# TensorE transposes for a few blocks of an attention layer, and output stores issued by SyncE

## Chip, cores and metric

The kernel runs on one core of one Trainium2 chip. A core has TensorE (PE, matrix products into PSUM), VectorE (DVE), ScalarE (ACT), GpSimd (POOL) and SyncE (SP, which here issues DMAs), and 16 DMA engines that all queues of the core share. Each engine executes its own instruction list in order and waits for the others by semaphores. The metric is device time in microseconds (us); less is better.

## What is computed

A decoder trunk of two layers over 2048 tokens of width 1024, in float32. Layer A is a gated linear recurrence; layer B is attention over a sliding window of 128 tokens, with 16 query heads of 64 and 2 shared key/value heads. The change concerns layer B alone:

```python
k, v = ...                            # computed once from layer A's output: projection, RMS norm per key head
h = rmsnorm(x, norm_g)
u = h @ w_in                          # 1024 -> 1024 queries | 1024 gates
q = rmsnorm(q per head, q_norm_g)
s = q @ k.T * scale + alibi           # per block of 128 queries: the block and the one before it, masked
p = exp(s - max) ; p = p / (sum(p) + exp(sink - max))
y = (p @ v) * silu(gate)
out = x + y @ w_out
```

## The kernel before

Every float32 operand is split into two float16 parts, hi and lo, and a product is three float16 passes (hi hi, hi lo, lo hi), accumulated in PSUM. Layer B works on 16 blocks of 128 tokens. For block b TensorE does:

- `project(b)`: keys and values (24 matmuls of 256 columns), then queries (48 of 512 columns); `project_gate(b)`: 48 of 512 columns; `finish(b)`: the output projection, 48 of 512 columns, which needs the transposed gated values `yT`.
- `scores(b, n)` for the two halves n of the heads (16 matmuls of 256 columns in 4 pairs of heads), which need the transposed queries `qT`; `values(b, n)` (32 small matmuls), which need the transposed exponentials `pT` and a masked copy of them that GpSimd makes.

A product needs its left operand with the contraction on the partitions, so normalized input, keys, queries, exponentials and gated values are transposed. All of these transposes are DMA transposes, issued on SyncE's queue by `flip` (line 321): per block one for xT, kT, qT and yT and two for pT; block 15 has two half ones for yT, since `finish(15)` is done in two parts. The block's residual input is loaded by SyncE (`fetch_chain`, line 1580, four buffers); the finished block is stored by GpSimd's queue (`x_add`, line 1888), except for block 15, whose halves SyncE stores (line 1885).

The order of the work is made at build time. `Plan` (line 81) holds the expected times of five engines. Each chain of steps (`q_chain`, `softmax`, `gate_chain`, ...) is a generator that yields what it will use, as `yield DVE_, 1220, 1` for an expected 1220 ns of DVE, `yield SP_, 1900` for the issue of a transpose, `yield None, 2500` for its landing, or a `Flag` to wait for. When several steps could begin, the one that can begin first goes first, and `RANK` breaks ties. TensorE is fed by two streams (`run`, line 142): `attention()` with scores and values, and `others()` with projections, gates and finishes; the first goes ahead whenever its flags are set by then, plus `SLACK` ns of margin. `LEAD`, `GAPS` and `TIMES` say how much TensorE time of the other stream has to pass before a step of attention may come; `LATER` moves `finish(12)`, `finish(13)` and `finish(14)` back in the order of the other stream. `end_plan` ties each engine's instructions to the order of the plan; on the chip an engine keeps that order whatever the real times are.

```python
seq.append(("finish", b - 1))               # 1540, behind project(b + 1) and gate(b + 1)
yield slot("s", 3), PAIR                    # 1487, one of 3 PSUM buffers for a pair of heads
yield SP_, 1900                             # 1783, in softmax
flip(ph.rearrange("p w h n -> p (w h n)"), pT.rearrange("p w h n -> p (w h) n"))
yield None, 2500
```

With `LATER = (1, 0, 1)` the end of the other stream is project(15), finish(12), gate(15), finish(13), finish(14), finish(15). `yT` has two buffers, so that block 14's is block 12's, and is free when `finish(12)` has been done. The gated values of all blocks pass through one buffer (`yS`), and so do their hi and lo parts (`yhl`).

Of the kernel before, what the change touches and what calls it, by code (L numbers as in the profile page):

```python
# [36 lines left out]

LEAD = 9353  # L40
PAIR, GAPS = 440, (1000, 800)
TIMES = ((4259, 2588, 17865, 17829), (2559, 6794, 2129, 5953), (19559, 3400, 24653, 13594), (14447, 15300, 0, 6800))
LATER = (1, 0, 1)


RANK = (4, 5, 3, 0, 1, 4, 2, 5, 3, 4, 0, 3, 5, 2)
SLACK = 300
LATE5 = 200
LO_POOL = (1, 2)

# [126 lines left out]
def trunk(ctx, tc, x, wA, gw, par, gains, woA, wkv, wB, woB, vec, alib, out):  # L177
# [12 lines left out]
    psum = [psA.enter_context(tc.tile_pool(name="psA", bufs=1, space=bass.MemoryType.PSUM))]  # L190


    id16 = xp.tile([P, P], F16, name="id16")
    make_identity(nc, id16)
    id32 = xp.tile([P, P], F32, name="id32")
    make_identity(nc, id32)
# [1280 lines left out]
    def scores(b, n):  # L1477
        d = st[b]
        yield [F["qT"][b], F["kT"][b]], 0
        if n == 0:  # L1480
            for k in ("rl", "lsum", "mr", "mt", "bi", "sk"):
                d[k] = col(k, HEADS)
            d["parts"] = 2 if b == NB - 1 else 1
        qT, kt = d["qT"], d["kT"]
        left = [4]
        for hp in range(4 * n, 4 * n + 4):
            yield slot("s", 3), PAIR
            o = pst([P, 2, 2 * P], F32, "s", uniq("s"), 3)
            free = taken("s")
            for i in range(2):  # L1490
                h = 2 * hp + i
                for w in range(2):
                    mm(o[:, i], qT[:, h], kt[:, h // 8, w].rearrange("p r n -> p (r n)"), w == 0, w == 1)
            plan.go(evacuate(b, n, hp, o, free, left), RANK[0])
            yield GAPS[0]
        H["s"][2 * b + n].set()
# [75 lines left out]
            f.set()  # L1572


    def fetch_chain(b):
        if b >= 4:
            yield st[b - 4]["stored"]
        yield SP_, 300
        xb = p3.tile([P, D], F32, tag="x1", name=uniq("x1"), bufs=4)
        nc.sync.dma_start(xb, x1D[b])  # L1580
        st[b]["x1"] = xb
        yield None, 3300
        F["x1"][b].set()

    def norm_chain():
# [27 lines left out]
    def kv_chain(b, kv, free):  # L1613
        d = st[b]
        yield ACT_, 650
        kn = p3.tile([P, 2, HD], F32, tag="kn", name=uniq("kn"), bufs=1)
        kss = col("kss", 2)
        for h in range(2):
            act.activation(kn[:, h], kv[:, h * 64 : h * 64 + 64], AF.Square, accum_out=kss[:, h : h + 1])
        yield DVE_, 230, 1  # L1620
        kva = col("kva", 2)
        dve.tensor_scalar(kva, kss, 1.0 / HD, epsk, ALU.mult, ALU.add)
        yield POOL_, 720
        rk = col("rk", 2)
        pool.tensor_tensor(rk, kva, mhalf[:, 0:2], ALU.pow)
        yield DVE_, 500
        for h in range(2):
            dve.scalar_tensor_tensor(kn[:, h], kv[:, h * 64 : h * 64 + 64], rk[:, h : h + 1], gk, ALU.mult, ALU.mult)
        yield ACT_, 270

        v32 = p3.tile([P, 2, HD], F32, tag="v32", name=uniq("v32"), bufs=2)
        act.activation(v32, kv[:, 128:256].rearrange("p (h d) -> p h d", h=2), AF.Copy, scale=2.0**-21)
        d["v32"] = v32
        free.set()
        plan.go(v_chain(b), RANK[10])
        yield ACT_, 500
        kd = p3.tile([P, 2, 2, 2, HD], F16, tag="kd", name=uniq("kd"), bufs=1)
        for r in range(2):
            act.copy(kd[:, :, 0, r], kn)
        yield POOL_, 900, 1  # L1640
        for r in range(2):
            pool.tensor_tensor(kd[:, :, 1, r], kn, kd[:, :, 0, 0], ALU.subtract)
        if b >= 2:
            yield H["s"][2 * b - 3]
        yield SP_, 1200
        kt = p3.tile([P, 2, 2, 2, P], F16, tag="kT", name=uniq("kT"), bufs=2)
        flip(kd.rearrange("p h w r d -> p (h w r d)"), kt.rearrange("p h w r n -> p (h w) r n")[:, :, 1, :])
        d["kT"] = kt
        yield None, 1700
        yield POOL_, 620, 1  # L1650
        if b == 0:
            pool.memset(kt[:, :, :, 0, :], 0.0)
        else:
            pool.tensor_copy(kt[:, :, :, 0, :], st[b - 1]["kT"][:, :, :, 1, :])
        F["kT"][b].set()
# [34 lines left out]
    def q_chain(b):  # L1690
        d = st[b]
        yield d["qparts"][0]
        yield d["qparts"][1]
        sq = qhS.rearrange("p h r d -> p (h r d)").bitcast(F32)
        qn, qh = qnS, qhS
        yield DVE_, 1210
        qss = col("qss", HEADS)
        dve.tensor_reduce(qss, sq.rearrange("p (h d) -> p h d", d=HD), AX.X, ALU.add)
        yield DVE_, 230, 1
        qva = col("qva", HEADS)  # L1700
        dve.tensor_scalar(qva, qss, 1.0 / HD, epsq, ALU.mult, ALU.add)
        yield POOL_, 2920
        rq = col("rq", HEADS)
        pool.tensor_tensor(rq, qva, mhalf, ALU.pow)
        yield POOL_, 220, 1
        rq2 = col("rq2", HEADS)
        pool.tensor_tensor(rq2, rq, qsc, ALU.mult)
        yield POOL_, 1900, 1
        pool.tensor_tensor(qn, qn, rq2.unsqueeze(2).to_broadcast([P, HEADS, HD]), ALU.mult)
        yield ACT_, 1050  # L1710
        act.copy(qh[:, :, 0], qn)
        yield DVE_, 1200, 1
        dve.tensor_tensor(qh[:, :, 1], qn, qh[:, :, 0], ALU.subtract)
        if b:
            yield H["s"][2 * b - 1]
        yield SP_, 1900
        qT = p3.tile([P, HEADS, P], F16, tag="qT", name=uniq("qT"), bufs=1)
        flip(qh.rearrange("p h r d -> p (h r d)"), qT)
        F["q"][b].set()
        d["qT"] = qT  # L1720
        yield None, 2900
        F["qT"][b].set()

    def g_part(b, n, o, free):
# [30 lines left out]
    def softmax(b, n):  # L1755
        s, d = sS, st[b]
        hs, i = bsf(n), 2 * b + n
        mr, mt, bi, sk, lsum, rl = (d[k][:, hs] for k in ("mr", "mt", "bi", "sk", "lsum", "rl"))
        vec = vecs[:, 128 + 8 * n : 136 + 8 * n]
        yield DVE_, 500, 1  # L1760
        dve.tensor_tensor(mt, mr, ssc[:, hs], ALU.mult)
        dve.tensor_tensor(mt, mt, vec, ALU.max)
        dve.tensor_scalar(bi, mt, -1.0, LN2_15, ALU.mult, ALU.add)  # L1763
        for h in range(8 * n, 8 * n + 8):
            yield ACT_, 480, 0, "exp"
            act.activation(  # L1766
                s[:, h],
                s[:, h],
                AF.Exp,
                bias=d["bi"][:, h : h + 1],  # L1770
                scale=ssc[:, h : h + 1],
                accum_out=d["lsum"][:, h : h + 1],
            )
        plan.go(row_sums(b, n), RANK[12])
        ph, pT = phS[n], pTs[n]
        if b:
            yield H["pv"][i - 2]
        yield DVE_, 700, 1
        dve.tensor_copy(ph[:, 0], s[:, hs])  # L1779
        yield DVE_, 1220, 1  # L1780
        dve.tensor_tensor(ph[:, 1], s[:, hs], ph[:, 0], ALU.subtract)  # L1781
        H["cut"][i].set()
        yield SP_, 1900
        flip(ph.rearrange("p w h n -> p (w h n)"), pT.rearrange("p w h n -> p (w h) n"))
        yield None, 2500
        H["pT"][i].set()
        for w in range(2):

            yield POOL_, 1090, 1
            pool.affine_select(ph[:, w], pT[:, w], [[0, 8], [-1, P]], ALU.is_gt, 0.0, base=0, channel_multiplier=1)  # L1790
        H["pU"][i].set()
# [38 lines left out]
    def gate_chain(b, i):  # L1830
# [24 lines left out]
        yh = yhl[:, 2 * i * n : 2 * (i + 1) * n]  # L1855
        if b and i == 0:
            yield F["yh"][b - 1]
        yield ACT_, 1150 / parts
        act.activation(yh[:, 0:n], yi, AF.Copy, scale=syb)
        yield DVE_, 1285 / parts, 1  # L1860
        dve.scalar_tensor_tensor(yh[:, n : 2 * n], yi, syb, yh[:, 0:n], ALU.mult, ALU.subtract)  # L1861
        if i == parts - 1:
            F["yfree"][b].set()
        if b >= 2 and i == 0:
            yield F["out"][b - 2]
        yield SP_, 1900
        if i == 0:
            d["yTt"] = p3.tile([P, 2 * KD, P], F16, tag="yT", name=uniq("yT"), bufs=2)
            d["yTp"] = flag()
        m = 2 * KD // parts  # L1870
        F["yh"][b].set()
        flip(yh, d["yTt"][:, i * m : (i + 1) * m])
        yield None, 2700
        (F["yT"][b] if i == 0 else d["yTp"]).set()

    def x_add(b, n, p, o, free):
# [5 lines left out]
        if d["parts"] == 2:  # L1882
            if p == 1:
                yield SP_, 300
                nc.sync.dma_start(out[b * P : (b + 1) * P, n * CH : n * CH + CH], sl)
        elif n == 1:
            yield POOL_, 640
            pool.dma_start(out[b * P : (b + 1) * P, :], d["x1"])
            yield None, 3300
            d["stored"].set()  # L1890

    for b in range(NB):
# [81 lines left out]
```

## Time and profile before

| | us |
|---|---|
| median of 3 runs (1538.58 to 1542.13) | 1538.91 |
| the profiled execution, its own time | 1536.42 |
| its span | 1534.7 |
| layer A and weights, up to TensorE's first matmul of layer B | 873.6 |
| layer B, from there to TensorE's last matmul | 657.1 |
| from there to the end of the span | 4.0 |

| engine | busy us | share of the span |
|---|---|---|
| TensorE | 1496.4 | 98% |
| VectorE | 1027.4 | 67% |
| ScalarE | 887.8 | 58% |
| GpSimd | 421.8 | 27% |

Busy time is the time in which an instruction of the engine was in flight. On an engine that is busy nearly throughout, what is left to look for are the few places where it waits, and how fast it runs; on the others, idle time matters only where TensorE waits for them. The granted clock is TensorE's, as a share of full speed.

### The profile page before, as it was taken

The numbers are of one execution on the slowest core, as the hardware profiler recorded it, in microseconds if no ns is written. First come the engines' busy times: TensorE is split into PE (matmuls) and PEld (weight loads), VectorE is DVE, ScalarE is ACT, GpSimd is POOL, SyncE is SP. The second block draws the span as 40 slices with busy tenths as digits, with TensorE's granted clock in tenths as the row PEclk, the third lists the DMA queues.
The fourth block names the chain that finished last, engine by engine and source line by source line (L and its number), as shares of the span: only waits on it lengthen the run. The fifth ranks groups of instructions, "written<-read, shape, count | busy, mean of one in ns | idle before, by whom it ended". The sixth has DMA issues, their size and how long they took to land. (4 is left out here: it accounts for less than half of the span.)

```text
span 1534.7 us, 23073 instructions
## 1 busy us (share of the span) xinstructions
PE 1496.4 (98%) x8503; PEld 746.8 (49%) x8503; DVE 1027.4 (67%) x2221; ACT 887.8 (58%) x1773; POOL 421.8 (27%) x578
## 2 busy tenths in 40 slices
PE   5999999999999999999999999999999999999997
PEld 5444444444444444444444455555555555555553
DVE  7578878778777766963247246766657656756774
ACT  6678667767766757510145167665556646646761
POOL 2232111111111121100000135544344444454532
PEclk9999999999999999999999999999999999999998
DMA  6664122022143212796258334444434544454434
GB/s 195 161 169 104 34 80 68 26 82 66 28 149 122 83 61 88 263 331 244 104 186 293 126 70 85 102 90 97 100 87 100 88 95 100 77 120 90 90 70 96
DMA packets 242545, 177.27 MB, mean 116 GB/s; under 512 B 205056, under 2 KB 215552, under 8 KB 242432
## 3 DMA queue, kind: packets, MB, share of 16 engines
q1 hardware_dynamic: 233984, 146.95, 37.0%
q0 software_dynamic: 8304, 28.84, 5.5%
q8 instruction: 66, 1.08, 0.3%
q14 instruction: 47, 0.39, 0.1%
q10 hardware_dynamic: 144, 0.01, 0.0%
HBM read 92.93 MB, written 29.36 MB: 80 GB/s over the span
## 5 line engine op out<-in xcount | busy, mean ns | idle before, releaser
L275 PEld LDWEIGHTS <-w 128*128 128x128 f16 x2448 | 233.6, 99 | 269.0 <-issue 9.8
L275 PE MATMUL pm<-wq,xT 128*128 128x512 f16 x1536 | 340.3, 379 | 2.6 <-ACT gg L1728 2.6
L275 PEld LDWEIGHTS <-xT 128*128 128x128 f16 x1920 | 186.7, 98 | 178.3 <-issue 2.8
L275 PE MATMUL pu<-xnT,w 128*128 128x512 f16 (+2 forms) x1296 | 259.4, 358 | 2.9 <-DMA xnT<-xs 1.9
L275 PE MATMUL pg<-xnT,w 128*128 128x512 f16 x1152 | 251.9, 379 | 0.0
L275 PE MATMUL po<-wo,xnT 128*128 128x512 f16 x1152 | 249.4, 379 | 0.5 <-ACT ri L744 0.5
L275 PEld LDWEIGHTS <-xnT 128*128 128x128 f16 x1152 | 112.6, 98 | 136.0 <-issue 0.9
L275 PE MATMUL pm<-xnT,yT 128*128 128x512 f16 x768 | 174.5, 382 | 1.6 <-DMA yT<-qy 1.6
L675 DVE SCALAR_TENSOR_TENSOR xc<-u,cwS,xc 128x512 f32<-128x512 f32 x144 | 110.7, 776 | 66.0 <-ACT xc L671 62.8
L1766 ACT ACTIVATE sq<-sq,bi,ssc 128x128 f32<-128x128 f32 x256 | 123.4, 486 | 7.2 <-DVE bi L1763 7.1
L275 PEld LDWEIGHTS <-yT 128*128 128x128 f16 x768 | 74.2, 98 | 86.4 <-DMA yT<-qy 1.7
L1739 ACT COPY sq<-s 128x256 f32<-128x256 f32 x128 | 47.2, 373 | 87.2 <-PE s L275 82.6
L300 ACT ACTIVATE xnT<-xnT,sy 128x1536 f16<-128x1536 f32 x14 | 22.0, 1570 | 128.4 <-PE po L275 128.4
L685 POOL TENSOR_TENSOR hl<-xc,hl 128x512 f16<-128x512 f32 x32 | 42.2, 1321 | 175.6 <-ACT hl L680 136.6
L734 ACT ACTIVATE gs<-pg,gsc 128x512 f32<-128x512 f32 x48 | 32.9, 688 | 95.9 <-DMA yD<-gs 68.7
L1741 DVE COPY_PREDICATED sq<-mask,s 128x256 f32<-128x256 int32 x128 | 53.0, 439 | 30.7 <-ACT sq L1739 29.6
L1750 DVE CUSTOM_DVE_ANT_0 sq<-sq,al 128x128 f32<-128x128 f32 x256 | 72.5, 329 | 0.1
L275 PE MATMUL pr<-hl,gw 128*128 128x512 f16 x288 | 68.2, 380 | 2.8 <-ACT gs L734 1.8
L744 ACT ACTIVATE ri<-pr,pr,rsc 128x512 f32<-128x512 f32 x96 | 69.4, 776 | 1.2 <-PE pr L275 0.7
L816 POOL DMA_DIRECT2D yD<-gs x48 | 36.8, 766 | 118.5 <-DVE gs L806 118.3
L275 PE MATMUL s<-kT,qT 128*128 128x256 f16 x512 | 67.2, 273 | 1.7 <-DMA qT<-qy 1.5
L1202 DVE SCALAR_TENSOR_TENSOR xnT<-po,cA,xnT 128x512 f32<-128x512 f32 x28 | 20.8, 748 | 70.6 <-PE po L275 70.6
(255 smaller groups left out, 2204.6 us busy)
## 6 DMA issues: line engine op xcount, KB each, us to landing
xnT<-in_wB_dram SPq DMA_DIRECT2D x32, 512.0 KB, 6.0
yD<-gs POOLq DMA_DIRECT2D x48, 256.0 KB, 2.8
st<-in_woA_dram SPq DMA_DIRECT2D x24, 512.0 KB, 4.3
xnT<-yD SPq DMA_DIRECT2D x16, 768.0 KB, 5.5
st<-in_wA_dram SPq DMA_DIRECT2D x15, 768.0 KB, 5.3
xs<-in_x_dram SPq DMA_DIRECT2D x16, 512.0 KB, 3.8
xnT<-in_x_dram SPq DMA_DIRECT2D x16, 512.0 KB, 5.0
x1D<-xnT POOLq DMA_DIRECT2D x16, 512.0 KB, 4.4
```

Of the source, the lines that this page charges most:

```text
L275: lastmm[0] = pe.matmul(o, lhsT, rhs, start=start, stop=stop, skip_group_check=True)
L300: act.activation(hi, src, AF.Copy, scale=scale)
L675: dve.scalar_tensor_tensor(xc, u[:, d : d + CH], cw[:, j, d : d + 1], xc, ALU.mult, ALU.add)
L685: (pool if j in LO_POOL else dve).tensor_tensor(hl[:, 1], xc, hl[:, 0], ALU.subtract)
L734: act.activation(gs, o, AF.Silu, scale=W["gsc"])
L744: act.activation(v, o[j], AF.Sigmoid, bias=pr[:, t0 + j, 5 + w : 6 + w], scale=W["rsc"])
L816: pool.dma_start(yD[4 * c : 4 * c + 4, :, t, :].rearrange("b p n -> p b n"), gs.rearrange("p (b n) -> p b n", n=P),)
L1202: dve.scalar_tensor_tensor(xs_, o[n], cA[:, c : c + 1], xs_, ALU.mult, ALU.add)
L1739: act.copy(sl, o[:, :, P:])
L1741: dve.copy_predicated(sl, mask.unsqueeze(1).to_broadcast([P, 2, P]), o[:, :, 0:P])
L1750: dve.tensor_tensor_reduce(s[:, h], s[:, h], al[:, i * P : (i + 1) * P], 1.0, -3.4e38, ALU.add, ALU.max, m)
L1766: act.activation(s[:, h], s[:, h], AF.Exp, bias=d["bi"][:, h : h + 1], scale=ssc[:, h : h + 1], accum_out=d["lsum"][:, h : h + 1],)
```

## The change

It is in layer B alone (`id16`, the identity that a TensorE transpose multiplies with, moves to a pool that lives through both layers).

- Transposes of block 0's queries, of both halves of block 15's exponentials and of the gated values of blocks 14 and 15 (`TURNED`) are done by TensorE, eight (block 15's gated values: four) 128x128 transposes into a PSUM buffer of the scores' ring; ACT copies the hi part out of PSUM and DVE the lo part. For exponentials and gated values the hi part's transposes are asked for as soon as the hi part is there.
- The stores of blocks 0 to 14 are issued by SyncE, where the transposes are issued.
- The plan counts a landing by a queue: each transfer lands no earlier than its own least time and a pitch behind the one before. The scores' step waits for its PSUM buffer in a loop, since transposes take from the same ring.
- `LEAD`, `GAPS`, `TIMES`, `LATER`, `RANK` and `SLACK` (300 to 800) have other values, so the order of all engines in layer B is another one. With `LATER = (3, 0, 4)` the end of the other stream is project(15), gate(15), finish(13), finish(12), finish(14), finish(15).

```diff
-LEAD = 9353
-PAIR, GAPS = 440, (1000, 800)
-TIMES = ((4259, 2588, 17865, 17829), (2559, 6794, 2129, 5953), (19559, 3400, 24653, 13594), (14447, 15300, 0, 6800))
-LATER = (1, 0, 1)
-RANK = (4, 5, 3, 0, 1, 4, 2, 5, 3, 4, 0, 3, 5, 2)
-SLACK = 300
+LEAD = 4247
+PAIR, GAPS = 440, (200, 0)
+TIMES = ((2559, 5094, 34030, 39052), (1700, 8506, 3406, 7647), (33135, 3406, 20406, 28900), (0, 50171, 12765, 21253))
+LATER = (3, 0, 4)
+RANK = (4, 5, 3, 0, 2, 4, 0, 4, 3, 1, 5, 3, 5, 0)
+SLACK = 800
+TURNED = ((0,), (15,), (14, 15))
...
+    LANDS = {"turn": (2450, 2350), "keys": (1250, 1150), "block": (2900, 1600)}
+    queue = [0.0]
+    def landing(kind):
+        least, rate = LANDS[kind]
+        queue[0] = max(plan.now + least, queue[0] + rate)
+        return queue[0] - plan.now
+    def turn(src, dest, n, engine, done):
+        free = None
+        while slot("s", 3) not in ([], [free]):
+            free = slot("s", 3)[0]
+            yield free
+        free = taken("s")
+        tp = pst([P, KD, P], F16, "s", uniq("tp"), 3)
+        yield None, SLACK
+        yield PE_, 64 * n
+        for i in range(n):
+            pe.transpose(tp[:, i], src[:, i * P : (i + 1) * P], id16)
+        if engine == DVE_:
+            yield DVE_, 60 + 80 * n
+            dve.tensor_copy(dest, tp[:, 0:n])
+        else:
+            yield ACT_, 200 + 100 * n
+            act.copy(dest, tp[:, 0:n])
+        free.set()
+        done.set()
...
+        if b in TURNED[0]:
+            fs = [flag() for _ in range(2)]
+            for i, e in enumerate((ACT_, DVE_)):
+                plan.go(turn(qf[:, i * D : (i + 1) * D], qT[:, KD * i : KD * (i + 1)], KD, e, fs[i]), RANK[5])
+            yield fs[0]
+            yield fs[1]
...
+        if b in TURNED[1]:
+            plan.go(turn(ph[:, 0].rearrange("p h n -> p (h n)"), pT[:, 0], KD, ACT_, fs[0]), RANK[11])
         yield DVE_, 1220, 1
         dve.tensor_tensor(ph[:, 1], s[:, hs], ph[:, 0], ALU.subtract)
...
+        if b >= 2 and i == 0 and b in TURNED[2]:
+            yield F["out"][b - 2]
...
         act.activation(yh[:, 0:n], yi, AF.Copy, scale=syb)
+        if b in TURNED[2]:
+            plan.go(turn(yh[:, 0:n], d["yTt"][:, i * m : i * m + m // 2], m // 2, ACT_, fs[0]), RANK[13])
         yield DVE_, 1285 / parts, 1
         dve.scalar_tensor_tensor(yh[:, n : 2 * n], yi, syb, yh[:, 0:n], ALU.mult, ALU.subtract)
...
-            yield POOL_, 640
-            pool.dma_start(out[b * P : (b + 1) * P, :], d["x1"])
-            yield None, 3300
+            yield SP_, 400
+            nc.sync.dma_start(out[b * P : (b + 1) * P, :], d["x1"])
+            yield None, landing("block")
             d["stored"].set()
```

## Rows read from the trace of the kernel before

**Rows 1.** The page's first part: busy us, share of span, instructions of each engine.
```profile
PE 1496.4 (98%) x8503; PEld 746.8 (49%) x8503; DVE 1027.4 (67%) x2221; ACT 887.8 (58%) x1773; POOL 421.8 (27%) x578
```
**Rows 2.** TensorE's waits in layer B: us in total, times, longest.
```profile
PE po L275 <- DMA ppx<-gg: 6.5, 3, 3.4
PE pm L275 <- ACT gg L1728: 2.6, 1, 2.6
PE pm L275 <- DMA yT<-qy: 1.6, 1, 1.6
PE s L275 <- DMA qT<-qy: 1.5, 1, 1.5
PE po L275 <- POOL gg L1790: 0.8, 2, 0.6
```
**Rows 3.** Timeline of TensorE: start, us, what, count, [idle before it <- releaser].
```profile
1231.58 0.51 PE L275 MATMUL po<-vt,ppx 128*128 128x128 f16 x8 [1.75 <-DMA ppx<-gg]
...
1502.94 0.82 PE L275 MATMUL po<-vt,ppx 128*128 128x128 f16 x8 [3.42 <-DMA ppx<-gg]
1505.35 3.59 PE L275 MATMUL pm<-xnT,yT 128*128 128x512 f16 x8 [1.58 <-DMA yT<-qy]
...
1515.02 15.70 PE L275 MATMUL pm<-xnT,yT 128*128 128x512 f16 x72
```
**Rows 4.** Busy time by stretch, one of the middle, two of the tail.
```profile
core 0: us, PE busy (x) PEld busy (x) DVE busy (x) ACT busy (x) POOL busy (x), PEclk, DMA share, GB/s
933.00:1229.00 296.00, 295.81 (x1987) 165.71 (x1985) 197.82 (x618) 183.37 (x522) 132.12 (x137) 1.00 0.46 93
...
1500.00:1505.00 5.00, 0.82 (x8) 0.67 (x8) 3.35 (x10) 0.42 (x2) 1.95 (x3) 0.79 1.14 210
1505.00:1510.00 5.00, 4.66 (x27) 2.45 (x28) 0.00 (x0) 0.33 (x1) 2.51 (x3) 0.53 0.80 194
```
**Rows 5.** Timeline of ScalarE where TensorE waits 2.6 us for it.
```profile
928.85 1.28 ACT L1728 ACT_TABLE_LOAD   x1
```
**Rows 6.** TensorE transposes of layer A, and their copies: timeline, then groups (busy, mean ns).
```profile
20.28 0.61 PE L884 MATMUL xt<-id,ri 128*128 128x128 f16 x8
20.73 0.83 PE L275 MATMUL pu<-xnT,w 128*128 128x128 f16 x12
...
21.06 0.99 ACT L888 COPY xnT<-xt 128x1024 f16<-128x1024 f16 x1
...
L891 DVE COPY xnT<-xt 128x1024 f16<-128x1024 f16 x4 | 2.7, 682 | 0.4 <-PE xt L884 0.3
...
L884 PE MATMUL xt<-id,ri 128*128 128x128 f16 x64 | 5.9, 250 | 2.9 <-DVE ri L875 1.4 <-ACT xnT L888 1.1 <-ACT ri L872 0.4
```
**Rows 7.** DMA issues of layer B: count, median us from issue to landing.
```profile
yT<-qy SPq DMA_TRANSPOSE x17, 4.3
...
ppx<-gg SPq DMA_TRANSPOSE x16, 4.7
```
**Rows 8.** A transpose and a store by GpSimd, twice: issues in time, and us to landing.
```profile
1063.49 0.64 POOL L1888 DMA_DIRECT2D out_dram<-x  x1
1063.77 4.02 SPq L321 DMA_TRANSPOSE ppx<-gg  x1
ppx<-gg SPq DMA_TRANSPOSE x1, 5.6
...
1223.23 1.31 SPq L321 DMA_TRANSPOSE ppx<-gg  x1
1223.42 0.64 POOL L1888 DMA_DIRECT2D out_dram<-x  x1
ppx<-gg SPq DMA_TRANSPOSE x1, 8.3
```
**Rows 9.** Timeline of the tail: how block 14's gated values are split into hi and lo.
```profile
1497.38 1.14 ACT L1859 ACTIVATE qy<-qy,syb 128x1024 f16<-128x1024 f32 x1
1498.87 1.27 DVE L1861 SCALAR_TENSOR_TENSOR qy<-qy,syb 128x1024 f16<-128x1024 f32 x1
```

More of the change, by code (lines that the diff above doesn't have):

```diff
@@ L190, in trunk @@
     psum = [psA.enter_context(tc.tile_pool(name="psA", bufs=1, space=bass.MemoryType.PSUM))]
-    id16 = xp.tile([P, P], F16, name="id16")
+    id16 = cp.tile([P, P], F16, name="id16")
     make_identity(nc, id16)
@@ L1484, in scores @@
         qT, kt = d["qT"], d["kT"]
-        left = [4]
+        left, free = [4], None
         for hp in range(4 * n, 4 * n + 4):
-            yield slot("s", 3), PAIR
+            while slot("s", 3) not in ([], [free]):
+                free = slot("s", 3)[0]
+                yield [free], 0
+            free = taken("s")
             o = pst([P, 2, 2 * P], F32, "s", uniq("s"), 3)
-            free = taken("s")
+            yield [], PAIR
             for i in range(2):
@@ L1572, in second_stream @@
             f.set()
+    LANDS = {"turn": (2450, 2350), "keys": (1250, 1150), "block": (2900, 1600)}
[6 more added lines that the diff above has]
+        free = None
+        while slot("s", 3) not in ([], [free]):
+            free = slot("s", 3)[0]
+            yield free
+        free = taken("s")
+        tp = pst([P, KD, P], F16, "s", uniq("tp"), 3)
[11 more added lines that the diff above has]
+        done.set()
     def fetch_chain(b):
@@ L1648, in kv_chain @@
         d["kT"] = kt
-        yield None, 1700
+        yield None, landing("keys")
         yield POOL_, 620, 1
@@ L1715, in q_chain @@
             yield H["s"][2 * b - 1]
-        yield SP_, 1900
+        if b not in TURNED[0]:
+            yield SP_, 1900
         qT = p3.tile([P, HEADS, P], F16, tag="qT", name=uniq("qT"), bufs=1)
-        flip(qh.rearrange("p h r d -> p (h r d)"), qT)
-        F["q"][b].set()
+        qf = qh.rearrange("p h r d -> p (h r d)")
         d["qT"] = qT
-        yield None, 2900
+        if b in TURNED[0]:
[4 more added lines that the diff above has]
+            yield fs[1]
+            F["q"][b].set()
+        else:
+            flip(qf, qT)
+            F["q"][b].set()
+            yield None, landing("turn")
         F["qT"][b].set()
@@ L1779, in softmax @@
         dve.tensor_copy(ph[:, 0], s[:, hs])
+        fs = [flag() for _ in range(2)]
+        if b in TURNED[1]:
+            plan.go(turn(ph[:, 0].rearrange("p h n -> p (h n)"), pT[:, 0], KD, ACT_, fs[0]), RANK[11])
         yield DVE_, 1220, 1
@@ L1782, in softmax @@
         H["cut"][i].set()
-        yield SP_, 1900
-        flip(ph.rearrange("p w h n -> p (w h n)"), pT.rearrange("p w h n -> p (w h) n"))
-        yield None, 2500
+        if b in TURNED[1]:
+            plan.go(turn(ph[:, 1].rearrange("p h n -> p (h n)"), pT[:, 1], KD, DVE_, fs[1]), RANK[11])
+            yield fs[0]
+            yield fs[1]
+        else:
+            yield SP_, 1900
+            flip(ph.rearrange("p w h n -> p (w h n)"), pT.rearrange("p w h n -> p (w h) n"))
+            yield None, landing("turn")
         H["pT"][i].set()
@@ L1857, in gate_chain @@
             yield F["yh"][b - 1]
+        if b >= 2 and i == 0 and b in TURNED[2]:
+            yield F["out"][b - 2]
+        m = 2 * KD // parts
+        if b in TURNED[2] and i == 0:
+            d["yTt"] = p3.tile([P, 2 * KD, P], F16, tag="yT", name=uniq("yT"), bufs=2)
+            d["yTp"] = flag()
+        fs = [flag() for _ in range(2)]
         yield ACT_, 1150 / parts
         act.activation(yh[:, 0:n], yi, AF.Copy, scale=syb)
+        if b in TURNED[2]:
+            plan.go(turn(yh[:, 0:n], d["yTt"][:, i * m : i * m + m // 2], m // 2, ACT_, fs[0]), RANK[13])
         yield DVE_, 1285 / parts, 1
@@ L1863, in gate_chain @@
             F["yfree"][b].set()
[L1864 to L1873, printed above, removed]
+        if b in TURNED[2]:
+            plan.go(turn(yh[:, n : 2 * n], d["yTt"][:, i * m + m // 2 : (i + 1) * m], m // 2, DVE_, fs[1]), RANK[13])
+            yield fs[0]
+            yield fs[1]
+            F["yh"][b].set()
+        else:
+            if b >= 2 and i == 0:
+                yield F["out"][b - 2]
+            yield SP_, 1900
+            if i == 0:
+                d["yTt"] = p3.tile([P, 2 * KD, P], F16, tag="yT", name=uniq("yT"), bufs=2)
+                d["yTp"] = flag()
+            F["yh"][b].set()
+            flip(yh, d["yTt"][:, i * m : (i + 1) * m])
+            yield None, landing("turn")
         (F["yT"][b] if i == 0 else d["yTp"]).set()
@@ L1886, in x_add @@
         elif n == 1:
-            yield POOL_, 640
-            pool.dma_start(out[b * P : (b + 1) * P, :], d["x1"])
-            yield None, 3300
+            yield SP_, 400
+            nc.sync.dma_start(out[b * P : (b + 1) * P, :], d["x1"])
+            yield None, landing("block")
             d["stored"].set()
```

## Prediction

> **What bounds the kernel.** I read engine shares first, then TensorE's waits, then the timeline around each wait, then the DMA landings. TensorE is busy for 98% of the span [rows 1], so the span can only shrink where TensorE waits, does less work, or runs at a lower clock. Layer A is untouched. In layer B TensorE's waits sum to 6.5 + 2.6 + 1.6 + 1.5 + 0.8 = 13.0 us [rows 2]. The reader should see where they lie. In the long middle there is next to none: 295.81 of 296 us are busy [rows 4]. At the start there are two, 1.5 us for block 0's transposed queries and 2.6 us for a PSUM buffer that ScalarE frees late. In the middle blocks there are two places, each a wait for a block's transposed exponentials (1.75 us in one [rows 3]; the three waits of that kind sum to 6.5 and the longest is 3.4, so the other is 1.3) with 0.8 us in all for the masked copy behind them: 3.9 us. In the tail there are 3.42 us for block 15's exponentials and 1.58 us for block 14's gated values, 5.0 us [rows 3].
>
> The tail has a second cost. Behind those waits the granted clock is 0.79 and then 0.53 of full speed, where it is 1.00 in the middle [rows 4]; 0.53 is nearly all at the lower level of 1.2 GHz. Eight matmuls take 3.59 us there, and 72 take 15.70 us later, 0.218 us each [rows 3], so eight should take 1.75: 1.8 us lost. The small ones between lose some 0.7 us more (0.82 against 0.51 for the same eight in the first and third of rows 3 is 0.3, and twice as many follow). I put the lost clock at 2.5 us. All that can be won is 13.0 + 2.5 = 15.5 us.
>
> **The change, part by part.**
>
> *Added work on TensorE.* Block 0's queries are 16 transposes, block 15's exponentials 32, block 14's gated values 16, block 15's 16: 80. Layer A has such transposes: a group of eight starts at 20.28 and the next matmul at 20.73, so 56 ns each in a row [rows 6]. 80 x 0.056 = 4.5 us. It is nearly all on the path, since TensorE is what bounds. The ten copies out of PSUM take 0.99 us on ScalarE or 0.68 us on VectorE at full size [rows 6]; these engines are 58% and 67% busy, and the copies stand only in the chains that I cost below.
>
> *Block 0's queries.* A DMA transpose of this size takes 4.3 to 4.7 us from issue to landing [rows 7]; eight transposes and their copy take 20.28 to 22.05, some 1.8 us [rows 6]. Two and a half us or more are saved on a chain that made TensorE wait 1.5 us, and the scores are now placed by when they can come, with 0.8 us of margin. I take the 1.5 us as won; from 0 to 1.5.
>
> *The 2.6 us for ScalarE.* There a gate's activation stands behind a key's square in ScalarE's order and needs a table load of 1.28 us [rows 5], while all three PSUM buffers of the products are taken. The change gives gates the first rank and brings scores earlier. But rank only breaks ties, and the exponentials that keep ScalarE busy ahead of it are still there. Between 0 and 2.6 I take half, 1.3 us.
>
> *Output stores on SyncE.* In one of the two middle waits GpSimd issued the 512 KB store 0.19 us after SyncE had issued the transpose, and the transpose took 8.3 us instead of the usual 4.7. Where the store came 0.28 us ahead of the transpose, the transpose took only 5.6 us [rows 8, 7]. In SyncE's own queue a store cannot be issued into the middle of an earlier transpose, and what is behind it pays 5.6 - 4.7 = 0.9 us, which the plan now counts. So the two middle waits go: 3.9 us, from 0 to 3.9. GpSimd loses 15 issues of 0.64 us that held up nobody. The new wait is VectorE's last addition of a block at the head of SyncE's list, with the next transposes behind it. Its cover is that TensorE does other blocks' products meanwhile, which is why almost nothing shows in the middle now; without it up to 0.9 us per block.
>
> The Trainium skill ("DMA: Bandwidth & Descriptors", section "Issuing engines are not separate DMA queues") says that DMAs of scalar, sync or gpsimd run on the same 16 DMA engines and interleave whichever engine started them, and that issuing elsewhere saves only sequencer time. By that rule the store would disturb as before and the sum would be 3.9 us higher. The two rows above differ by the order of issue, which speaks for an effect of the order, but no run here has the store in SyncE's queue.
>
> *Tail.* The work that fills it is reordered: gate(15) now comes ahead of finish(12), so block 15's scores start some 10 us of TensorE work earlier relative to the end, and finish(13) and finish(12) (48 matmuls each, 48 x 0.218 = 10.5 us) lie between gate(15) and finish(14). Before, only finish(13) did. Block 15's softmax also loses its DMA landing. So the 3.42 us go, with the 1.58 behind them and the lower clock: 7.5 us. What is late next is block 14's yT: it takes block 12's buffer, and finish(12) is now the last before finish(14). In the plan ScalarE's hi part, VectorE's lo part, the transposes and the copy follow finish(12): 1.14 + 1.27 [rows 9] + 0.45 + 0.68 [rows 6], with hand-overs some 4.0 us, of which TensorE transposes 0.9: 3.1 us idle. But hi and lo themselves need only yhl, which is free, so if ScalarE and VectorE come to them early, there remain the last copy and its hand-overs, about 1 us; with block 15's values in between, nothing. I take 1.5 us, from 0 to 3.1.
>
> *Sum.* Won 1.5 + 1.3 + 3.9 + 7.5 = 14.2; added 4.5 + 1.5 = 6.0; net 8.2 us. Against the profiled execution, 1536.42 us (span 1534.7 and 1.7 around it), that is 1528.2. The median of the runs shown is 1538.91, 2.5 us above it; what is timed is a median, so I forecast 1538.9 - 8.2 = 1530.7. Its own range: 15.5 - 4.5 = 11.0 gives 1527.9 at best, and with 1.3 us more from ScalarE and 1.6 from yT it is 1533.6.
>
> **Rivals.**
>
> 1. *The store collides from SyncE's queue too.* Then the 3.9 us stay: 1534.6, and with the two open terms at their worse ends 1537.5. For it: one store and one transpose share the same DMA engines. Against: the two orders of issue above. 0.20.
> 2. *Block 14's yT becomes the tail's wait at the lower clock.* 1.6 us more of waiting and the 2.5 us of clock back: 1530.7 + 4.1 = 1534.8. For it: finish(12) stands right ahead of finish(14). Against: its wait is broken up by transposes and the values. 0.07.
> 3. *The places change, the sum of waits does not:* the new order makes as many waits of its own as it removes, and the transposes come on top: 1538.9 + 4.5 = 1543.4, less the 2.5 us or so that the shorter chains give: 1540.9. Against: the old order, with 0.3 us of margin, ran the middle without waits. 0.06.
> 4. *Slower: SyncE's list is held up.* A store whose addition is late, or that lies ahead of a block's exponentials, delays their landing by 0.9 us [rows 7, 8] plus the wait, and TensorE waits in the block. At 0.9 us for the landing and as much again for the wait at the head, 1.8 us for 15 blocks are 27 us: 1558. It decides from 1543.5 on, (1543.5 - 1530.7) / 1.8, that is from 7 or 8 of the 15 blocks; 10 blocks give 1549. Against: the loads of the same size stand in that list already, and the middle has no waits. 0.07.
> 5. *Slower: transposes do not overlap.* Each takes 250 ns by its own duration [rows 6]; without overlap 80 cost 20.0 instead of 4.5 us: 1546.2. Against: eight in 0.45 us. 0.02. The Trainium skill ("TensorE: Matmul & The Clock Gate", "Part 4: PE-mode transpose") gives about 275 ns for one in a kernel's context; by it the sum would be 17.5 us higher, 1548. Layer A's row shows that it is no rate.
>
> **How the numbers follow.** About 0.3% is what a measurement of this kernel can tell from no change: below 1534.3 is faster, above 1543.5 slower. The forecast has 0.58, all of it faster; rival 1 gives 0.05 and rival 2 gives 0.03 of theirs to faster, where an open term comes out better. Faster 0.66. Same: 0.15 + 0.04 + 0.06 = 0.25. Slower: 0.07 + 0.02 = 0.09. The range takes in the forecast, rivals 1 and 2, and at the lower end 1.4 us for the scatter of the medians (the runs differ by 3.6 us): 1526.5 to 1537.5.
>
> **What the profile after would show.** Eighty new matmuls near 56 ns apart, in groups of eight or four. At the start no wait for block 0's queries. In the middle blocks no transpose above about 6 us and no store issue on GpSimd; a wait for exponentials in more than two blocks would be rival 4. Between finish(12) and finish(14) a wait of 0 to 3 us, and a granted clock of 1.00 to the end. If the tail still has a wait of 3 us ahead of values or finish(15), the step that says finish(12) fills it is wrong. If TensorE's busy time grows by more than 4.5 us at full clock, the price of a transpose is wrong.

## The result, and the profile after

The changed kernel takes 1526.91 us (median of five runs, 1525.31 to 1528.59) where the kernel before, in as many runs beside it, takes 1538.58. The ratio is 0.9929, with a 95% interval from 0.9908 to 0.9949. The forecast was 1530.7 in a range from 1526.5 to 1537.5, with faster as the likeliest outcome. A second measurement of the same kernel (e11 below) gave 0.9928 (0.9914 to 0.9942). Of all runs shown, one is far off, at 3212 us in e6, and its ratio leaves it out.

The profiled execution has a span of 1525.0 us where it was 1534.7. I measure layer B from the start of TensorE's first key matmul to the end of its last matmul: 657.1 us before (873.60 to 1530.73) and 648.8 after (872.29 to 1521.05). So 8.4 us of the 9.7 lie in layer B. The other 1.3 us are layer A, which is taken up below.

The engines' shares on the page, to be read beside [rows 1], and TensorE's waits in layer B, to be read beside [rows 2] (us in total, times, longest):

```profile
PE 1495.1 (98%) x8583; PEld 748.8 (49%) x8583; DVE 1024.3 (67%) x2227; ACT 891.5 (58%) x1779; POOL 414.5 (27%) x563
```
```profile
PE s L277 <- DVE sq L1786: 1.3, 1, 1.3
PE s L277 <- DMA qT<-qy: 1.0, 1, 1.0
PE tp L1600 <- DVE qy L1923: 1.0, 1, 1.0
PE po L277 <- DMA ppx<-gg: 0.8, 1, 0.8
PE pm L277 <- ACT yT L1606: 0.2, 1, 0.2
```

TensorE has 80 more matmuls and yet no more busy time. Its waits went from 13.0 to 4.3 us. The two long ones, for ScalarE's gate and for block 15's exponentials, are not in the list any more. What is there is new or small: scores that wait for a PSUM buffer of their ring, block 1's queries, the low part of block 14's gated values (line 1923 is the split, 1600 the transposes), one wait for exponentials in a middle block.

The tail by stretch (busy time, then PEclk, DMA share and GB/s in the last three columns; the last two are the windows of [rows 4]), and TensorE's timeline where block 14's gated values and block 15's exponentials are turned (start, us, what, count, idle before):

```profile
1490.00:1500.00 10.00, 8.83 (x95) 5.83 (x94) 8.33 (x16) 7.65 (x23) 3.16 (x3) 1.00 0.14 54
1500.00:1505.00 5.00, 5.00 (x36) 2.62 (x34) 3.90 (x13) 1.48 (x3) 3.15 (x3) 1.00 0.00 2
1505.00:1510.00 5.00, 5.00 (x56) 3.19 (x54) 3.43 (x8) 1.76 (x4) 0.00 (x0) 1.00 0.01 3
```
```profile
1481.05 1.47 PE L277 MATMUL s<-kT,qT 128*128 128x256 f16 x12
...
1483.72 8.80 PE L277 MATMUL pm<-xnT,yT 128*128 128x512 f16 x40
1492.36 1.06 PE L1600 MATMUL tp<-id,gg 128*128 128x128 f16 x16
1493.25 0.61 PE L1600 MATMUL tp<-id,qy 128*128 128x128 f16 x8
1494.84 0.62 PE L1600 MATMUL tp<-id,qy 128*128 128x128 f16 x8 [0.98 <-DVE qy L1923]
1495.30 0.50 PE L277 MATMUL po<-vt,ppx 128*128 128x128 f16 x8
1495.99 2.76 PE L277 MATMUL pm<-xnT,yT 128*128 128x512 f16 x12 [0.19 <-ACT yT L1606]
```

The granted clock is 1.00 to the end, where it was 0.79 and 0.53. Behind finish(12), whose last matmuls begin at 1483.72, stand the transposes. TensorE waits once, 0.98 us, for the low part of block 14's gated values, and 0.19 us for a copy. Sixteen transposes in a row take 1.06 us.

### The profile page after: what moved, and what is told of

Its sections match the earlier page's. It is cut to its first block, busy times and chain, and to the rows that moved or that the text cites. A ratio compares the mean times of both kernels' runs of the same rounds, so it can differ in the third digit from the quotient of the medians.

```text
span 1525.0 us, 23216 instructions
## 1 busy us (share of the span) xinstructions
PE 1495.1 (98%) x8583; PEld 748.8 (49%) x8583; DVE 1024.3 (67%) x2227; ACT 891.5 (58%) x1779; POOL 414.5 (27%) x563
## 4 chain that ended last, share of the span: by engine, by line
PE 91%; DVE 3%; DMA 3%; ACT 2%; issue 1%; POOL 0%; SPq 0%; ACTq 0%; DVEq 0%
PE pm L277 34%; PE po L277 19%; PE pu L277 15%; PE pg L277 14%; PE pr L277 5%; PE s L277 4%; DMA yD<-gs 1%; DMA ppx<-gg 1%; DVE amx L418 0%; ACT sq L1811 0%; DMA xnT<-xs 0%; DMA st<-in_wA_dram 0%; DMA qT<-qy 0%; PE f2b L239 0%; DVE ri L790 0%
## 5 line engine op out<-in xcount | busy, mean ns | idle before, releaser
L687 POOL TENSOR_TENSOR hl<-xc,hl 128x512 f16<-128x512 f32 x32 | 42.2, 1321 | 174.3 <-ACT hl L682 135.3
L1795 DVE CUSTOM_DVE_ANT_0 sq<-sq,al 128x128 f32<-128x128 f32 x256 | 68.9, 316 | 0.1
```

Source lines behind the costliest of these rows:

```text
L687: (pool if j in LO_POOL else dve).tensor_tensor(hl[:, 1], xc, hl[:, 0], ALU.subtract)
L1795: dve.tensor_tensor_reduce(s[:, h], s[:, h], al[:, i * P : (i + 1) * P], 1.0, -3.4e38, ALU.add, ALU.max, m)
```

## The experiments

Each kernel's layer B is measured as above; the waits are TensorE's in layer B, summed from its list. The ratio is to the kernel before on the same chip. Before, e2, e3 and e9 have the old constants of the plan, the others the new ones.

| kernel | ratio, 95% interval | layer B us | waits us |
|---|---|---|---|
| before | 1 | 657.1 | 13.0 |
| after | 0.9929 (0.9908 to 0.9949) | 648.8 | 4.3 |
| e1: after, stores on GpSimd | 0.9944 (0.9931 to 0.9956) | 647.2 | 2.8 |
| e2: before, stores on SyncE | 0.9963 (0.9949 to 0.9976) | 653.6 | 8.7 |
| e3: before, identity kept | 1.0003 (0.9994 to 1.0012) | 658.3 | 12.9 |
| e4: after, no TensorE transposes | 1.0013 (1.0004 to 1.0023) | 659.7 | 14.9 |
| e5: after, queries by DMA | 0.9952 (0.9935 to 0.9968) | 650.4 | 5.0 |
| e6: after, exponentials by DMA | 0.9961 (0.9947 to 0.9975) | 651.8 | 6.4 |
| e7: after, gated values by DMA | 0.9954 (0.9934 to 0.9974) | 651.0 | 6.6 |
| e8: after, old order of finishes | 0.9940 (0.9923 to 0.9956) | 648.1 | 3.1 |
| e9: after, old constants | 1.0010 (1.0000 to 1.0020) | 659.7 | 12.7 |
| e10: after, block 1's queries turned too | 0.9929 (0.9913 to 0.9945) | 648.1 | 2.6 |
| e11: after, once more | 0.9928 (0.9914 to 0.9942) | 647.8 | 3.5 |

**e1, the store's queue, from after.**

```diff
-            nc.sync.dma_start(out[b * P : (b + 1) * P, :], d["x1"])
+            pool.dma_start(out[b * P : (b + 1) * P, :], d["x1"])
```


> The changed kernel with one edit: blocks 0 to 14 are stored from GpSimd's queue again; the plan still counts the store as SyncE's, so every other instruction keeps its place. Theory (the order in SyncE's queue protects the transposes): some transposes of 7 to 8 us beside a store come back, with waits for exponentials in the middle blocks, 2 to 5 us in all; layer B 651 to 654 us where the changed kernel has 648.8, the median 2 to 5 us above the changed kernel's 1526.9. Rival 1 (a store collides from either queue, or the new places avoid the collision by themselves): layer B within 1 us of 648.8, the median within 1.5 us of 1526.9.

Layer B is 647.2 us and the median 1527.16: the rival, though layer B lies 1.6 us below 648.8 where it allowed 1. (The changed kernel once more, e11, has 647.8.) The new order does not need the store in SyncE's queue. The store still delays a transpose when the two meet, but here it meets gated values, for which nobody is pressed: the six transposes issued within 2 us behind a store took 4.6 to 6.9 us, where the same six took 4.3 to 5.5 after the change. For the longest, below, the packets in the trace show the store's ahead of the transpose's, which begin some 0.8 us later than in a transpose without a store; what made the rest of the 6.9 us is open. The issue by GpSimd, SyncE's issue of the transpose 0.75 us later, and the transpose's landing (last number, us):

```profile
1336.14 0.64 POOL L1955 DMA_DIRECT2D out_dram<-x  x1 [12.18 <-DVE mr L1795]
```
```profile
1336.89 3.42 SPq L323 DMA_TRANSPOSE yT<-qy  x1
```
```profile
yT<-qy SPq DMA_TRANSPOSE x1, 6.9
```

**e2, the store's queue, from before.**

```diff
-            pool.dma_start(out[b * P : (b + 1) * P, :], d["x1"])
+            nc.sync.dma_start(out[b * P : (b + 1) * P, :], d["x1"])
```


> The kernel before with one edit: the stores of blocks 0 to 14 are issued by SyncE, at the place in the order that the old plan gave them on GpSimd. Theory: the two middle waits (4.5 us counted from start to start of TensorE's instructions) go and at most 1 us comes new; layer B 652 to 654 us where the kernel before has 657.1, the median 3 to 5 us below the kernel before. Rival 1 (a store collides from SyncE's queue too): layer B within 1 us of 657.1. Rival 4 (the list is held up by stores that wait for VectorE): waits in many blocks, layer B above 661 us.

Layer B falls to 653.6 us and the time by 0.37%: the theory (the median fell by 6.0 us, 1 us more than it said), and rivals 1 and 4 of the prediction fall with it. In one of the blocks that waited before, the store now goes ahead of the exponentials, which land in 4.9 us, where it was 7.9 (in the other, 8.3 [rows 8]). Issues in time, then the landing; below them TensorE's waits that are left:

```profile
1341.36 0.54 SPq L1888 DMA_DIRECT2D out_dram<-x  x1
1342.06 3.27 SPq L321 DMA_TRANSPOSE ppx<-gg  x1
```
```profile
ppx<-gg SPq DMA_TRANSPOSE x1, 4.9
```
```profile
PE po L275 <- DMA ppx<-gg: 3.6, 2, 3.4
PE pm L275 <- ACT gg L1728: 2.6, 1, 2.6
PE pm L275 <- DMA yT<-qy: 2.1, 1, 2.1
PE s L275 <- DMA qT<-qy: 0.4, 1, 0.4
```

The middle's two waits are gone; start and tail together cost 1.2 us more than before, counted from start to start. The packets in the trace show what happened to the exponentials. Before, in the stretch from 1225 to 1230.5 of the transpose that took 8.3 us, the store's packets (first line, with 16 small ones) and the transpose's (second line) lie among one another. In e2, in the same block, the 128 packets of the store come first (third line, 1222.5 to 1224.05) and nearly all of the transpose's behind them (fourth line, 1224.2 to 1226.7). Queue, packets, MB and share:

```profile
q0 software_dynamic: 144, 0.52, 42.7%
q1 hardware_dynamic: 1403, 0.36, 73.7%
```
```profile
q1 hardware_dynamic: 128, 0.52, 101.1%
```
```profile
q1 hardware_dynamic: 2044, 0.55, 118.6%
```

The Trainium skill says ("DMA: Bandwidth & Descriptors", "Queues, rings and completion order") that each DMA engine takes turns between the queues that have work for it; the packets agree. By the Trainium skill ("DMA: Bandwidth & Descriptors", "Issuing engines are not separate DMA queues"), issuing elsewhere saves only sequencer time; e2 against the kernel before does not bear that out. But e2 moved the store ahead of the transpose as well as to another queue. Where GpSimd's own store came 0.28 us ahead, in the 5.6 us case of [rows 8], its packets came first too, so that the order matters in any case, and how much the queue adds no run separates cleanly; the six transposes of e1, 4.6 to 6.9 us against 4.3 to 5.5 with much the same order, are the nearest to it.

**e3, the identity's place.**

```diff
-    id16 = xp.tile([P, P], F16, name="id16")
+    id16 = cp.tile([P, P], F16, name="id16")
```


> The kernel before with one edit: the float16 identity lies in the pool that lives through both layers. In the profiled executions layer B starts at 873.60 us before and at 872.29 us after the change, though layer A's work is the same. Theory (scatter of layer A from one execution to the next): layer B's start between 872 and 875 us, the median within 2 us of the kernel before. Rival (the place of the identity, and of what lies behind it in memory, saves 1.3 us in layer A): layer B's start near 872.3 us, the median 1.3 us below.

The ratio is 1.0003 and layer B starts at 874.4 us. The place shows no effect. Over all the profiled executions of this study layer B starts between 871.8 (e2) and 875.3 us (e10), so 1.3 us there is scatter.

**e4, no transposes on TensorE.**

```diff
-TURNED = ((0,), (15,), (14, 15))
+TURNED = ((), (), ())
```


> The changed kernel without any TensorE transpose: queries, exponentials and gated values go through DMA transposes again; new plan constants and SyncE stores stay, and the plan is made again for it. TensorE does 4.5 us less. Theory (the shorter chains are what removes the waits at the start and in the tail): waits of 8 to 13 us at the start and in the tail, the granted clock below 1.00 in the tail, layer B 654 to 658 us, the median 5 to 9 us above the changed kernel's. Rival (the order of the finishes alone fills the tail): waits as after the change, layer B 643 to 647 us, the median 2 to 5 us below the changed kernel's.

Layer B is 659.7 us and the time 0.13% above the kernel before: the theory, and more. The new order without the transposes loses. TensorE's long waits on its timeline, and the granted clock around the second (0.66):

```profile
1499.40 6.18 PE L277 MATMUL pm<-xnT,yT 128*128 128x512 f16 x20 [4.62 <-DMA yT<-qy]
1520.12 4.12 PE L277 MATMUL pm<-xnT,yT 128*128 128x512 f16 x10 [5.78 <-DMA yT<-qy]
```
```profile
1514.00:1524.00 10.00, 4.22 (x12) 1.44 (x11) 4.25 (x13) 1.44 (x2) 0.00 (x0) 0.66 0.41 105
```

**e5, e6 and e7, one group of transposes at a time back to DMA.** The edits are `TURNED = ((), (15,), (14, 15))`, `((0,), (), (14, 15))` and `((0,), (15,), ())`.

> The changed kernel, but block 0's queries go through a DMA transpose; the plan is made again. TensorE does 16 transposes (0.9 us) less. Theory (the early queries also remove the 2.6 us wait for ScalarE's gate activation, since with the older chain it came back without any transposes): 1 us for the queries and 2.6 us for the gate are waited at the start, followed by a lower clock; layer B 649.5 to 652 us. Rival (the gate's wait was removed by its new rank, and came back only through the rest of that order): no wait for the gate, layer B 647 to 649 us.

> The changed kernel, but block 15's exponentials go through DMA transposes; the plan is made again. TensorE does 32 transposes (1.8 us) less. Theory (finish(13) and finish(12) cover the exponentials' chain, transposed either way): layer B 646 to 648.5 us, the median 0 to 2 us below the changed kernel's 1526.9. Rival (the wait of 3.4 us for exponentials in the old tail was the landing's): a wait of 2 to 4 us ahead of block 15's values with a lower clock behind it, layer B 650 to 654 us.

> The changed kernel, but the gated values of blocks 14 and 15 go through DMA transposes; the plan is made again. TensorE does 32 transposes (1.8 us) less. Theory (the two long waits for gated values in the tail without any transposes, 4.8 and 5.9 us, are theirs alone, as finish(12) stands right ahead of finish(14) and nothing covers a landing there): both come back with a lower clock behind them, layer B 656 to 661 us. Rival (they came from the late exponentials of that run): at most one wait under 2 us, layer B 646 to 650 us.

In e5 the wait for ScalarE's gate is back, at full length and with a clock of 0.83 in the ten us around it, though the gate has its new rank:

```profile
PE pm L277 <- ACT gg L1773: 2.6, 1, 2.6
```
```profile
925.00:935.00 10.00, 7.39 (x39) 3.64 (x37) 3.67 (x10) 5.14 (x12) 5.11 (x6) 0.83 1.15 198
```

It is there in every kernel that has block 0's queries transposed by DMA (before, e2 to e5) and absent or at 0.3 us in every one that turns them (after, e1, e6 to e11). So the early queries remove it. In the order of ScalarE it is plain why. After the change the gate's table load (line 1773) comes at 923.08, ahead of the next block's key squares (line 1654); in e5 it comes behind them, and those have to wait for TensorE. After, then e5:

```profile
923.08 1.28 ACT L1773 ACT_TABLE_LOAD   x1
924.38 1.50 ACT L1773 ACTIVATE gg<-pm,gscB 128x512 f32<-128x512 f32 x2
927.81 0.22 ACT L1654 ACTIVATE kn<-pm 128x64 f32<-128x64 f32 x1 [1.00 <-PE pm L277]
```
```profile
926.15 0.22 ACT L1654 ACTIVATE kn<-pm 128x64 f32<-128x64 f32 x1 [1.80 <-PE pm L277]
...
926.69 1.28 ACT L1773 ACT_TABLE_LOAD   x1
```

e6 is for its rival: waits of 1.3 us and less for exponentials and transposes pile up in the tail, and the clock falls to 0.57 of full speed in the stretch behind them:

```profile
1495.00:1503.00 8.00, 6.42 (x32) 3.08 (x33) 4.54 (x5) 1.89 (x6) 4.30 (x3) 0.57 0.69 163
```

e7 lies between its theory (656 to 661 us) and its rival (646 to 650): waits for gated values do come back, but 2.8 us in two, not the 10.4 of e4. So it takes more than their own landing to make the long ones. In e4 the transpose of block 14's was issued 2.3 us later than in e7 (1495.08 and 1492.76), yet ahead of the exponentials' transposes; that these were the cause is not shown. By these three, each group is worth some 2 to 4 us of layer B, after its own transposes are paid.

**e8, the order of the finishes.**

```diff
-LATER = (3, 0, 4)
+LATER = (1, 0, 1)
```


> The changed kernel with LATER as before: finish(12) ahead of gate(15), then finish(13), finish(14), finish(15); the rest of the constants, the transposes and the stores stay, and the plan is made again. Theory of the prediction (the 10.5 us of finish(12) moved behind gate(15) fill the hole of the tail): a wait of 2 to 5 us ahead of block 15's values, layer B 651 to 655 us. Rival (the transposes' shorter chains remove the tail's waits in either order): layer B within 1.5 us of 648.8, and the wait between finish(12) and finish(14) gone or moved.

Layer B is 648.1 us with waits of 3.1 us: the rival. finish(12) ahead of gate(15) or far behind it, the tail is the same. All of TensorE's waits in layer B, of which the last three lie in the tail:

```profile
PE po L277 <- DMA ppx<-gg: 1.1, 2, 0.8
PE s L277 <- DMA qT<-qy: 1.0, 1, 1.0
PE pm L277 <- ACT yT L1606: 0.4, 1, 0.4
PE tp L1600 <- DVE ph L1824: 0.3, 1, 0.3
PE tp L1600 <- ACT ppx L1606: 0.3, 1, 0.3
```

**e9, the old constants.** All six constants of the kernel before, with `TURNED` and the stores as after the change.

> The changed kernel with LEAD, GAPS, TIMES, LATER, RANK and SLACK of the kernel before; transposes by TensorE for the same blocks, SyncE stores and the loop for the scores' buffers stay, and the plan is made again. Theory (the transposes pay only in an order made for them: the new order without them was no faster than the old kernel, and the old places hold attention back until set amounts of other work have passed, whatever comes earlier): waits of 6 us or more remain in the last two blocks, layer B 655 to 662 us. Rival (the transposes remove the waits of the start and the tail in any order, as they did with either order of the finishes): waits under 3 us at the start and in the tail, layer B 648 to 651 us.

Layer B is 659.7 us, in the range of the theory, and a wait of over 6 us stands in one of the last two blocks, as it said. But that wait is a new one and none of those that were to remain, and the tail is clean, as the rival said: from block 15's scores on, no wait is above 0.4 us. What costs is one wait in block 14, for queries that still go by DMA. It and the lower clock behind it take 10.4 us, counted from start to start. The wait, GpSimd's scaling of these queries, and the issue of their transpose:

```profile
1448.66 3.60 PE L276 MATMUL s<-kT,qT 128*128 128x256 f16 x16 [8.41 <-DMA qT<-qy]
```
```profile
1439.19 1.90 POOL L1743 TENSOR_TENSOR sq<-sq,rq 128x1024 f32<-128x1024 f32 x1
```
```profile
1444.29 1.32 SPq L322 DMA_TRANSPOSE qT<-qy  x1
```

Their chain ran late: GpSimd scaled them behind masked copies of the block before, and the DMA transpose was issued only at 1444.29. Why the old constants place it so in the new plan I have not taken apart.

**e10, block 1's queries too.** `TURNED = ((0, 1), (15,), (14, 15))`.

> The changed kernel, but block 1's queries are turned by TensorE too, to remove the wait of 1.2 us for them that stands in each profile with the new constants; the plan is made again. Theory (a wait on TensorE is worth its length, a transpose its 56 ns): 1.2 us less waiting, 0.9 us more work, layer B 647 to 649 us, the median within 1.5 us of the changed kernel's. Rival (turning more queries also moves ScalarE and VectorE, which copy, into the way of block 0's softmax): new waits at the start, layer B 650 us or more.

The wait is gone and 0.9 us of work has come: layer B 648.1 us. It is as fast as the change, not faster. **e11** is the changed kernel once more.

> The changed kernel itself once more, beside the others on one chip. Theory (the 2.5 us by which its median gained more than its layer B is scatter of layer A and of the runs): layer B 647 to 649.5 us, its start anywhere from 871.5 to 874.5 us, a ratio to the kernel before from 0.993 to 0.996. Rival (a real gain outside layer B): layer B's start near 872.3 us and a ratio at or below 0.993.

Layer B is 647.8 us, starting at 873.9: the theory for the start, though the ratio comes out at the rival's edge. The median gained 10 us here, layer B 9.3 us against the profile before.

## Why the prediction held, and where it did not

The sum said 8.2 us and layer B's profile shows 8.4. Its parts are less exact than that. For their sizes I add up, over all matmuls of layer B, the time between one's start and the next's beyond the usual pitch for its columns (216, 109, 56 and 29 ns for 512, 256, 128 and 64): 18.7 us before and 5.8 after, where I had put 15.5 as the most that could be won. What was won is taken before rounding.

| us | forecast | before to after |
|---|---|---|
| start (queries and gate) | 2.8 won | 4.6 to 3.0: 1.5 won |
| middle blocks | 3.9 won | 5.9 to 0.9: 5.0 won |
| tail, clock and new wait included | 6.0 won | 7.6 to 1.5: 6.1 won |
| differences below 40 ns each | none | 0.6 to 0.4: 0.3 won |
| 80 transposes | 4.5 lost | 4.5 lost |

*What bounds, and the price of a transpose: right.* Layer A's 56 ns is what the tail shows, sixteen in 1.06 us. Rival 5 falls: one transpose is on record for 219 ns and eight for 0.61 us together, because they overlap. The Trainium skill ("TensorE: Matmul & The Clock Gate", "Part 4: PE-mode transpose") gives about 275 ns for one in a kernel; as the price of each in a row, that figure does not hold here.

*Start: the wrong half.* I took the whole 1.5 us for the queries and half of the 2.6 us for the gate. The gate's wait went entirely; e5 shows that the early queries did it, not the rank. The other part was not foreseen: with scores placed earlier, two other waits come, 1.3 us for a PSUM buffer of the scores and 1.0 us for block 1's queries. In e1, whose order differs from the changed kernel's in the store alone, the first of these does not show, so it is not there in every execution.

*Stores: right mechanism, wrong credit.* e2 shows that a store put into SyncE's own queue, ahead of the exponentials, spares them, as argued from the two orders of issue [rows 8]; they land in 4.9 us, 0.7 us sooner than the 5.6 that I took. But in the new order the stores fall where they hurt nobody, and e1 is as fast. The middle's gain is real, and either the queue or the order gives it. It came out 1.1 us above my 3.9: counted from start to start the two waits are 4.5 us, a handful of gaps of 0.1 to 0.3 us that the list of waits mostly leaves out adds 1.4, and 0.9 us is left. Nothing showed of rival 4.

*Tail: the size was right and the reason wrong.* The failed step is "finish(13) and finish(12) ... lie between gate(15) and finish(14). Before, only finish(13) did. ... So the 3.42 us go". e8 puts finish(12) back and loses nothing. Block 15's scores did not keep their place behind gate(15): before, they began ahead of its last matmuls, after, 11 us behind its end. So they did not come earlier relative to the end either: they ended 42.2 us before TensorE's last matmul in the profile before (1488.50 to 1530.73), and 38.7 us after (1482.36 to 1521.05), taking as their end the start of what follows them:

```profile
1487.19 1.47 PE L275 MATMUL s<-kT,qT 128*128 128x256 f16 x12
1488.50 1.89 PE L275 MATMUL pm<-xnT,yT 128*128 128x512 f16 x8
```
```profile
1481.05 1.47 PE L277 MATMUL s<-kT,qT 128*128 128x256 f16 x12
1482.36 0.50 PE L277 MATMUL po<-vt,ppx 128*128 128x128 f16 x8
```

The work behind them is the same to 1 us, 42.2 - 7.6 = 34.6 us before and 38.7 - 1.5 - 3.6 (64 transposes) = 33.6 after. Moving a finish past a gate here only permuted what stands ahead of the scores. What filled the hole is the other thing that I named in passing, the shorter chains: e6 and e7 bring waits and the low clock back, one group at a time, and e9 has a clean tail with the old order. The 1.5 us that I took for block 14's gated values were 0.98 + 0.19 us, but not by the cheap variant of the two. ScalarE began the hi part as finish(12) ended, and VectorE the lo part 1.0 us behind that:

```profile
1492.05 1.13 ACT L1919 ACTIVATE qy<-qy,syb 128x1024 f16<-128x1024 f32 x1
1493.54 1.25 DVE L1923 SCALAR_TENSOR_TENSOR qy<-qy,syb 128x1024 f16<-128x1024 f32 x1
```

From finish(12) to finish(14) it took 3.6 us (1492.36 to 1495.99), near the 4.0 of the dear variant. It was cheap because TensorE had work in between: sixteen transposes of block 15's exponentials and a group of its values.

*Constants.* The prediction counted the new order as part of each item and never asked what either half does alone. The new constants without the transposes (e4) and the transposes without the constants (e9) are each no faster than the kernel before, and some 6 us slower in layer B than e2, which has neither; together they are 5 us faster than e2. That does not show that the transposes need these constants: without the one wait in block 14 and the clock behind it, e9's layer B would be 659.7 - 10.4 = 649.3 us, an estimate, about the changed kernel's. How the gain divides between the two stays open.

*The 2 to 4 us by which the medians gained more than forecast.* Layer B's 8.4 to 9.3 us are most of the 10 to 12 us between medians. The rest has no place in the profiles. e3 and the starts of layer B, which scatter over 3.5 us, speak for scatter rather than for a gain in layer A; that it is nothing else is not shown.

## What to carry to other kernels

Where the main engine is busy throughout, work added to it can pay if it shortens a chain where nothing covers that chain, here the first and the last blocks: 4.5 us of transposes, with an order made for them, removed 7.6 us of waits and low clock there. To say what fills a hole in the tail, count the work that stands behind the step that the tail waits for; reordering what is ahead of that step does not change it. And an order tuned for one set of latencies has to be remade when they change: half of such a change, tried alone, can look like a loss, in e9 by a single wait.

## What the runs showed of the hardware

- Where GpSimd's 512 KB store was issued 0.19 us behind a DMA transpose on SyncE's queue, the packets of both lay among one another for about 5 us, and the transpose took 7.9 and 8.3 us where 4.3 or 4.7 is usual. Where the store's packets came first, it took 5.6 us (GpSimd's queue, 0.28 us ahead) and 4.9 (SyncE's, 0.70 us ahead).
- The lower clock came with waits that were broken up by a little work, too: in e6 none of the waits in the tail was above 1.3 us on the list, and the clock fell to 0.57. In the changed kernel a tail with 0.98 and 0.19 us kept it at 1.00.
